# One layer trunk on one core: the c results of a block product in PSUM tiles of their own, no longer in the right half of the b tile

## The chip, the core and the metric

The kernel runs on one core of one Trainium2 chip. The metric is the time of one execution on the device in microseconds (us). Five engines work from queues of their own: TensorE (PE in the profile, with its weight loads as PEld), VectorE (DVE), ScalarE (ACT), GpSimd (POOL) and SyncE (SP, which issues most DMAs). Matmul results go to PSUM, and only DVE and ACT empty it here.

## The reference, cut to what matters

Two layers on 1024 tokens of width 1024, all in float32:

```
u = rms_norm(h);  proj = u @ w_in
mixed = concat(forgetting_attention(...), gated retention(...))
h = h + mixed @ w_out                                   # output projection
up = rms_norm(h) @ w_up                                 # 1024 x 5632
h = h + (gelu(conv(up[:, :2816])) * up[:, 2816:]) @ w_down
h = h + sigmoid(rms_norm(h) @ w_ple_gate) * (p @ w_ple_proj)
...
return rms_norm(h)
```

The change touches the products with w_out, w_up, w_down, and w_ple_gate of the first layer. The projections w_in, the attention, the retention, the embedding product and the gate of the second layer are left as they are.

## The kernel before, in words

Activations lie feature by token: a tile [128, 1024] holds 128 features of all tokens. Float32 precision is reached with two reduced parts, hi and lo, of each operand, and three matmuls (hi hi, hi lo, lo hi) for one product.

The four products named above go through `g_parts` (line 468). It computes a block of 256 output features by 1024 tokens, seen as a 2 x 2 matrix of 128 x 512 pieces c11, c12, c21, c22, with a scheme that needs seven multiplications of halves in place of eight. The seven are called parts and run in the order of NAMES (line 301): b0, c1, b1, c2, b2, a, b3. Parts b0 to b3 add up one after the other in one accumulator; each is emptied into the output pieces after it is computed, and the next goes on adding to what stands there. Parts c1 and c2 do so in a second accumulator, and part a stands alone. So b1 must wait until b0 has been emptied, b2 until b1 and b3 until b2 have, and c2 until c1 has.

Of PSUM there are two tiles `d` of 1024 columns (`dpsum`, line 175) and four tiles `s` of 512 columns (`spsum`, line 178). Before the change a block takes one d: its left half is the accumulator of the b parts, its right half that of the c parts. Part a takes an s. The attention's and retention's small products, and the statistics of the norms (`Stats.finish`, line 541), take tiles s too.

A part is 3 x len(moving) matmuls of 128 x 128 by 512 columns, where `moving` lists the pairs of contracted tiles: 2 in the output projection, 4 in up and gate, 3 or 2 in down. Over both layers there are 16 blocks of the output projection, 44 of up, 32 of down and 4 of the gate, 96 in all. `Joined` and `Stored` (lines 330 and 372) make the moving operands (x for part b0, xh and xl for the others) and `Fixed` (line 402) the weights (w, and wh and wl): sums of weights on POOL (tile ws), the hi part on ACT, the lo part on DVE. `Line` (line 445) loads and makes the weights of one block while the block before it is computed.

Emptying a part is `join` (line 496) where a product is added to h: one DVE addition of 128 x 512 for each piece. For the others it is `form` (line 503): b0 and b1 are copied by ACT (COPY), c1 by ACT with scale -1 (ACTIVATE), c2, b2 and a are added on DVE, and b3 is scaled into its piece on DVE. In the up stage the blocks named a (first half of up) and z (second half) take turns; in the gate they are named sg.

The code is traced in program order. The framework's scheduler then writes the queue of each engine, with a model of times (`schedule_with_timeline_sim=True`), and may move an instruction ahead of another on the same engine where no dependency and no tile forbids it; it writes the semaphore waits as well. SBUF is given out in 50 rooms and 6 half rooms (class Arena), and the order of their users is fixed. The output projection of a layer begins while the last retention pair is still running: `weave` mixes the two in the trace.

Of the kernel before, what the change touches and what calls it, by code (L numbers as in the profile page):

```python
# [19 lines left out]
T = 1024  # L20
# [139 lines left out]
def trunk(ctx, tc, ap):  # L160
# [11 lines left out]
    def G(name, dt=F32, shape=(P, T)):  # L172
        return arena.take(name, dt, shape)

    def dpsum():
        return ps.tile([P, T], F32, name="d", tag="d", bufs=2)

    def spsum():
        return ps.tile([P, 512], F32, name="s", tag="s", bufs=4)
# [54 lines left out]
    def weights():  # L234
        if len(ahead) < 2:
            fetch()
        return ahead.pop(0)
# [18 lines left out]
    def dense_fm(w, x):  # L256
        got = []
        for _ in g_dense_fm(w, x, got):
            pass
        return got[0]  # L260
# [207 lines left out]
    def g_parts(line, moving, evac, after=None):  # L468


        w = line.take()
        d = dpsum()
        for part, name in enumerate(NAMES):
            o = spsum() if name == "a" else d[:, 512:T] if name[0] == "c" else d[:, 0:512]
            more = name in ("b1", "b2", "b3", "c2")
            for p, x in enumerate(moving):
                whi, wlo = w.of(part, p)
                xhi, xlo = x.of(part)
                first, last = p == 0 and not more, p == len(moving) - 1
                nc.tensor.matmul(o, whi, xhi, start=first, stop=False, skip_group_check=more)  # L480
                nc.tensor.matmul(o, whi, xlo, start=False, stop=False, skip_group_check=more)
                nc.tensor.matmul(o, wlo, xhi, start=False, stop=last, skip_group_check=more)
                del whi, wlo, xhi, xlo
            evac(name, o)
            if part % 2 == 0:
                w.x[part // 2] = None
                if after:
                    after(part // 2)
                line.step()
            yield 0.7 * len(moving)  # L490

    def parts(*a):
        for _ in g_parts(*a):
            pass
# [413 lines left out]
    for l in range(DEPTH):  # L908
# [143 lines left out]
        def g_out():  # L1052

            nonlocal line, u, rb
            u = rb = None
            del pr[:], ret_tab[:]
            line = Line(specs())
            for p in range(2):
                mx.append(Joined(mixed[2 * p], mixed[2 * p + 1]))
                mixed[2 * p:2 * p + 2] = [None, None]  # L1060
            for q in range(4):
                for m in (2 * q, 2 * q + 1):
                    h[m] = G("h")
                    nc.sync.dma_start(h[m], h_dram[m])
                to = h[2 * q:2 * q + 2]
                yield from g_parts(line, mx, lambda name, s: join(name, s, to))
# [5 lines left out]
        for name in ("qs", "ks"):  # L1072
            d = dense_fm(weights(), u)
# [44 lines left out]
        for j in range(FC // 2):  # L1118
# [11 lines left out]
            for i in range(2):  # L1130
                c = G("conv")
# [9 lines left out]
            c = None  # L1141
# [6 lines left out]
            def after(n):  # L1148
                for m in u:
                    m.drop(n)  # L1150
                for m in stored[0]:
                    m.build(n)
                    if n < 3:
                        m.load(n + 1)
# [106 lines left out]
    for at, n in PIECES:  # L1261
        t = slice(at, at + n)
        pstats = Stats(n)
        for m in range(KC):
# [4 lines left out]
            d = dpsum() if m % 2 else spsum()  # L1269
# [3 lines left out]
            for i in range(parts):  # L1273
                c = slice(i * n // parts, (i + 1) * n // parts)
# [99 lines left out]
```

## Time and profile before

| | us |
|---|---|
| median of 3 runs | 3019.79 |
| lowest and highest | 3009.69 and 3020.57 |
| the profiled execution | 3013.45 |
| its span, first to last instruction | 3011.7 |

Stages, by what PE and DVE do: layer 0 attention and retention to about 502 us of the span, the output projection from 545 to 675 (until about 605 among the last of retention), up to 1147, down to 1425, gate to 1540; layer 1 attention to 2007, output projection to 2180, up to 2653, down to 2905, then the second gate and the final norm. In a row of the trace, every instruction has line 145, since a helper there records all of them, so rows are told apart by tile: `d<-xh,wh` is a matmul that writes a tile d from moving operand xh and weight wh. The idle time of an engine stands behind an instruction, with what ended it.

### The profile page before, as it was taken

How to read it: one execution, taken by the hardware profiler on the slowest of the kernel's cores; microseconds unless marked ns; L12 is line 12 of the kernel's file. 1: busy time of each engine (PE TensorE's matmuls, PEld its weight loads, DVE VectorE, ACT ScalarE, POOL GpSimd, SP SyncE). 2: the span in 40 equal slices, each digit the busy share in tenths (PEclk: the TensorE clock that was granted, in tenths of full speed). 3: DMA queues.
4: the chain of work that ended last, by engine and by line, in shares of the span. 5: the costliest groups of instructions: out<-in, count | busy, mean ns of one | idle time of the engine just before them, and what ended most of it. 6: DMA issues, size and time to landing. Idle time of an engine off the chain costs nothing.

```text
span 3011.7 us, 36343 instructions
## 1 busy us (share of the span) xinstructions
PE 2751.0 (91%) x13718; PEld 2257.8 (75%) x13718; DVE 2080.4 (69%) x3031; ACT 1227.8 (41%) x1824; POOL 885.5 (29%) x652
## 2 busy tenths in 40 slices
PE   8998999979999998997889889999699999989988
PEld 7887988747777776775678879887477777767766
DVE  4566656796777677779735656568967776777676
ACT  4454533453333333335434545334433333434252
POOL 2222232222332222333432222322223323223230
PEclk9999999989999998999999999999899999999999
DMA  5333123322332235433433331232222322364242
GB/s 154 85 85 91 45 80 100 106 88 74 109 107 93 88 126 192 142 104 108 169 104 85 85 91 45 80 106 96 87 84 98 112 88 94 137 207 129 84 140 95
DMA packets 116865, 315.77 MB, mean 105 GB/s; under 512 B 13521, under 2 KB 34513, under 8 KB 116689
## 3 DMA queue, kind: packets, MB, share of 16 engines
q1 hardware_dynamic: 113616, 305.05, 31.5%
q10 hardware_dynamic: 3072, 8.39, 1.2%
q8 instruction: 108, 1.77, 0.2%
q14 instruction: 69, 0.56, 0.1%
HBM read 210.04 MB, written 69.80 MB: 93 GB/s over the span
## 4 chain that ended last, share of the span: by engine, by line
PE 33%; DVE 12%; DMA 5%; issue 3%; ACT 3%; POOL 3%; SPq 0%; POOLq 0%; DVEq 0%; ACTq 0%
PE d L145 24%; PE s L145 8%; DVE wl L145 3%; POOL ws L145 2%; DVE xl L145 2%; DVE h L145 2%; DMA wr<-in_wup_dram 1%; DVE conv L145 1%; DVE t L145 1%; DMA zz<-zd 1%; ACT wh L145 1%; DVE ssq L145 1%; DMA wr<-in_wdown_dram 1%; DVE w L145 1%; DMA dr<-in_wtm_dram 0%
## 5 line engine op out<-in xcount | busy, mean ns | idle before, releaser
L145 PE MATMUL d<-xh,wh 128*128 128x512 f32 x1560 | 638.2, 409 | 81.8 <-DVE h L145 50.0
L145 PE MATMUL d<-xl,wh 128*128 128x512 f32 x1560 | 625.0, 401 | 0.2 <-DVE xl L145 0.2
L145 PE MATMUL d<-xh,wl 128*128 128x512 f32 x1560 | 623.9, 401 | 0.5 <-DVE wl L145 0.5
L145 POOL TENSOR_TENSOR ws<-wr 128x512 f32<-128x512 f32 (+2 forms) x192 | 267.3, 1401 | 1145.0 <-PE d L145 477.4
L145 PEld LDWEIGHTS d<-xh,wh 128*128 128x128 f32 x1560 | 299.4, 192 | 192.1 <-DVE h L145 52.0
L145 PEld LDWEIGHTS d<-xh,wl 128*128 128x128 f32 x1560 | 299.6, 192 | 72.6 <-DVE wl L145 1.5
L145 PEld LDWEIGHTS d<-xl,wh 128*128 128x128 f32 x1560 | 300.1, 192 | 65.8 <-DVE xl L145 0.6
L145 POOL TENSOR_TENSOR ws<-ws,wr 128x512 f32<-128x512 f32 (+2 forms) x192 | 270.8, 1411 | 129.1 <-issue 69.2
L145 PE MATMUL d<-x,w 128*128 128x512 f32 x936 | 243.2, 400 | 31.1 <-ACT w L145 12.0
L145 ACT CAST wh<-ws 128x1024 fp32r<-128x1024 f32 (+2 forms) x192 | 169.6, 888 | 229.5 <-POOL ws L145 220.6
L145 DVE TENSOR_TENSOR h<-h,d 128x512 f32<-128x512 f32 x288 | 194.8, 681 | 83.0 <-PE d L145 76.3
L145 DVE TENSOR_TENSOR wl<-ws,wh 128x1024 fp32r<-128x1024 f32 (+2 forms) x192 | 209.8, 1097 | 50.8 <-ACT wh L145 41.5
L145 PE MATMUL d<-dh,uh 128*128 128x256 f32 (+1 forms) x768 | 220.9, 289 | 19.7 <-DVE vst L145 10.3
L145 PEld LDWEIGHTS d<-x,w 128*128 128x128 f32 x936 | 174.7, 190 | 83.4 <-ACT w L145 18.3
L145 PE MATMUL d<-dl,uh 128*128 128x256 f32 (+1 forms) x768 | 220.0, 287 | 0.0
L145 PE MATMUL d<-dh,ul 128*128 128x256 f32 (+1 forms) x768 | 219.7, 287 | 0.0
L145 PE MATMUL d<-uh,dh 128*128 128x512 f32 (+1 forms) x584 | 197.2, 407 | 23.7 <-ACT dh L145 11.1
L145 POOL TENSOR_TENSOR dl<-dr,dh 128x1024 fp32r<-128x1024 f32 (+2 forms) x51 | 125.8, 2468 | 243.7 <-ACT dh L145 212.5
L145 PE MATMUL d<-ul,dh 128*128 128x512 f32 (+1 forms) x584 | 193.6, 398 | 0.6 <-DVE ul L145 0.6
L145 PE MATMUL d<-uh,dl 128*128 128x512 f32 (+1 forms) x584 | 190.7, 396 | 0.3 <-POOL dl L145 0.2
L145 PEld LDWEIGHTS d<-dh,uh 128*128 128x128 f32 x768 | 147.0, 192 | 22.2 <-DVE vst L145 10.7
L145 PE MATMUL s<-xh,wh 128*128 128x512 f32 x312 | 128.4, 413 | 35.9 <-ACT wh L145 26.0
(209 smaller groups left out, 5443.8 us busy)
## 6 DMA issues: line engine op xcount, KB each, us to landing
wr<-in_wup_dram SPq DMA_DIRECT2D x88, 512.0 KB, 3.6
zz<-zd SPq DMA_DIRECT2D x66, 512.0 KB, 4.1
wr<-in_wdown_dram SPq DMA_DIRECT2D x48, 384.0 KB, 4.0
zd<-z SPq DMA_DIRECT2D x66, 256.0 KB, 2.0
dr<-in_wqk_dram SPq DMA_DIRECT2D x32, 512.0 KB, 3.5
hs<-h SPq DMA_DIRECT2D x24, 512.0 KB, 2.6
h<-hs SPq DMA_DIRECT2D x24, 512.0 KB, 4.4
zd<-t SPq DMA_DIRECT2D x22, 512.0 KB, 2.6
```

The costliest lines, as they stand in the source:

```text
L145: ins = f(*[bare(v) for v in a], **{n: bare(v) for n, v in k.items()})
```

## The change

A block now takes only the left half of a d, for its b parts. Part c1 takes a tile s, which c2 uses again; part a takes another s, as before. The order in the trace, the matmuls and the emptying stay as they were. The right half of d is not used by blocks any more; the number of tiles d and s is unchanged.

```diff
         w = line.take()
-        d = dpsum()
+        b, c = dpsum()[:, 0:512], None
         for part, name in enumerate(NAMES):
-            o = spsum() if name == "a" else d[:, 512:T] if name[0] == "c" else d[:, 0:512]
+            if name in ("c1", "a"):
+                o = spsum()
+                c = o if name == "c1" else c
+            else:
+                o = c if name == "c2" else b
             more = name in ("b1", "b2", "b3", "c2")
```

## Rows read from the trace of the kernel before

**Rows 1.** The page's head: busy time of each engine with its share of the span and its instructions, and the shares of the chain that ended last by engine.

```profile
PE 2751.0 (91%) x13718; PEld 2257.8 (75%) x13718; DVE 2080.4 (69%) x3031; ACT 1227.8 (41%) x1824; POOL 885.5 (29%) x652
PE 33%; DVE 12%; DMA 5%; issue 3%; ACT 3%; POOL 3%; SPq 0%; POOLq 0%; DVEq 0%; ACTq 0%
```

**Rows 2.** The table by stretches: from and to, length, then busy us (and instructions) of PE, PEld, DVE, ACT and POOL, the granted clock of TensorE, the DMA share and GB/s. End of the output projection of layer 0, up of layer 0, last group of down of layer 0, end of the output projection of layer 1, up of layer 1.

```profile
600.00:675.00 75.00, 53.80 (x195) 36.34 (x193) 71.94 (x95) 37.47 (x53) 19.05 (x16) 0.91 0.25 88
675.00:1147.00 472.00, 441.71 (x1859) 347.70 (x1857) 345.44 (x343) 175.97 (x214) 143.83 (x89) 0.98 0.29 102
1366.00:1425.00 59.00, 41.49 (x145) 27.47 (x144) 58.65 (x76) 32.79 (x47) 20.46 (x14) 0.94 0.38 129
2105.00:2180.00 75.00, 54.40 (x193) 37.94 (x193) 71.20 (x94) 37.48 (x53) 19.35 (x16) 0.89 0.25 88
2180.00:2653.00 473.00, 443.72 (x1868) 349.62 (x1869) 351.70 (x348) 179.92 (x218) 144.92 (x89) 0.98 0.30 104
```

**Rows 3.** Waits of PE over the whole span: the tile that PE was to write, the engine and the tile it waited for, us in total, times, longest us.

```profile
PE d L145 <- DVE h L145: 54.0, 48, 4.6
PE s L145 <- ACT wh L145: 26.0, 21, 4.0
...
PE s L145 <- DVE wl L145: 13.0, 19, 1.5
...
PE s L145 <- ACT xh L145: 9.8, 5, 4.0
...
PE d L145 <- ACT z L145: 9.5, 14, 1.4
PE s L145 <- DVE xl L145: 9.0, 4, 4.1
...
PE d L145 <- ACT sg L145: 7.3, 5, 2.7
...
PE d L145 <- ACT a L145: 5.8, 10, 0.7
...
PE d L145 <- DVE z L145: 5.1, 7, 0.9
...
PE d L145 <- DVE a L145: 1.5, 2, 0.9
```

**Rows 4.** The same list for single stretches, the row of DVE's h alone, in this order: 502 to 605 (output projection beside retention, layer 0), 605 to 675 (its end), 1147 to 1366 (down of layer 0), 1366 to 1425 (its last group), 2007 to 2110 and 2110 to 2180 (output projection of layer 1, beside retention and its end), 2653 to 2905 (down of layer 1).

```profile
PE d L145 <- DVE h L145: 5.0, 5, 1.8
...
PE d L145 <- DVE h L145: 8.5, 6, 3.9
...
PE d L145 <- DVE h L145: 7.5, 10, 1.9
...
PE d L145 <- DVE h L145: 10.0, 7, 3.2
...
PE d L145 <- DVE h L145: 5.1, 5, 1.9
...
PE d L145 <- DVE h L145: 8.0, 5, 4.6
...
PE d L145 <- DVE h L145: 9.8, 10, 3.3
```

**Rows 5.** The order of time in the up stage of layer 0, from 741 to 764 us: start, duration, engine, operation, tiles, and in brackets the idle time before it with what ended it. Of a part of 12 matmuls only the first stands here.

```profile
741.49 0.58 ACT L145 COPY z<-d 128x512 f32<-128x512 f32 x1
742.69 0.39 PE L145 MATMUL s<-xh,wh 128*128 128x512 f32 x1
743.48 0.67 DVE L145 TENSOR_TENSOR a<-a,d 128x512 f32<-128x512 f32 x1
745.43 0.40 PE L145 MATMUL d<-xh,wh 128*128 128x512 f32 x1
751.18 0.60 ACT L145 ACTIVATE z<-d 128x512 f32<-128x512 f32 x1 [0.70 <-PE d L145]
751.66 0.68 DVE L145 TENSOR_TENSOR a<-a,d 128x512 f32<-128x512 f32 x1
751.84 0.50 PE L145 MATMUL d<-xh,wh 128*128 128x512 f32 x1 [0.69 <-ACT z L145]
754.94 0.59 ACT L145 COPY z<-d 128x512 f32<-128x512 f32 x1 [3.16 <-PE d L145]
763.24 0.67 DVE L145 TENSOR_TENSOR z<-z,d 128x512 f32<-128x512 f32 x1
763.96 0.50 PE L145 MATMUL d<-xh,wh 128*128 128x512 f32 x1 [0.74 <-DVE z L145]
```

**Rows 6.** Groups of instructions: line, engine, operation, tiles, shape and count, then busy us, mean ns of one, and the idle time before them with what ended it.

```profile
L145 PE MATMUL d<-xh,wh 128*128 128x512 f32 x1560 | 638.2, 409 | 81.8 <-DVE h L145 50.0
...
L145 DVE TENSOR_TENSOR h<-h,d 128x512 f32<-128x512 f32 x288 | 194.8, 681 | 83.0 <-PE d L145 76.3
...
L145 PE MATMUL s<-xh,wh 128*128 128x512 f32 x312 | 128.4, 413 | 35.9 <-ACT wh L145 26.0
```

**Rows 7.** All waits of all engines over the span, the largest: who waited, for whom, us in total, times, longest.

```profile
POOL ws L145 <- PE d L145: 526.0, 39, 28.9
```

**Rows 8.** The order of time beside retention in layer 0: the first and the last reading of one retention result in a tile s (its mean, and the result less its mean).

```profile
554.83 0.68 DVE L145 TENSOR_REDUCE gmean<-s 128x8 f32<-128x512 f32 x1
...
567.67 0.68 DVE L145 TENSOR_TENSOR yn<-s,gmean 128x512 f32<-128x512 f32 x1
```

## The prediction

> **What bounds the kernel now.** I read the page's totals first, then the table of stages, then who TensorE waited for, and last a stretch of the order of time. The totals say where to look: PE is busy for 2751 of 3011.7 us, and the chain that ended last gives PE 33% and DVE 12%, the largest two shares [rows 1]. So there are about 260 us of idle PE, and a change pays if it takes some of them away without adding others. In the up stage of a layer PE is idle for 30 us of 472, DVE for 127; in the end of the output projection, and in the last group of the down stage of layer 0, it is DVE that has nothing left: 71.9 of 75, 71.2 of 75 and 58.65 of 59 us [rows 2].
>
> The list of PE's waits has two kinds [rows 3]. Some are on operands (wh, wl, xh, xl: 26.0 + 13.0 + 9.8 + 9.0 = 57.8 us on the parts that go to s alone). The others are on the engine that empties PSUM: h by DVE 54.0, z by ACT 9.5, sg by ACT 7.3, a by ACT 5.8, z by DVE 5.1, a by DVE 1.5, together 83.2 us. Some 1.4 of the 54.0 belong to the last phase, which g_parts has no hand in (the window without it shows 9.8 us), so the pool that the change can touch is about 82 us, 2.7% of the span.
>
> **Do the two halves wait on each other?** All depends on this, and the order of time answers it [rows 5]. In that stretch z is the block that begins. Its b0 was emptied by the COPY at 741.49, over at 742.07. Its c1, in the other half, ended and was emptied by the ACTIVATE at 751.18, over at 751.78. At 751.84 PE starts a part that had been waiting for exactly that; the COPY at 754.94, started as that part ends, shows it to be b1. But b1 goes into b0's half, which had been empty for nearly 10 us: it waited for the other half. The same at 763.96: DVE's add at 763.24 empties one of c2 and b2, the next part of the block waits for it, and whichever of the two it is, its own half was emptied at 751.18 or 754.94. So in this build a tile's halves are handed back and forth as one thing. A block is a chain of six parts and six emptyings, b0 c1 b1 c2 b2 b3, and PE has work only because two blocks, with a tile d each, run side by side. That is seen too: at 742.69 PE takes part a of z, the later block, ahead of b2 of a at 745.43, which became free when DVE emptied c2 (743.48 + 0.67).
>
> The Trainium skill, "PSUM — Partial Sum Buffer", Summary: rules for kernel authors, says that to read PSUM while a matmul runs one should target another bank, and guard with semaphores by bank. By that, halves that are banks already would need no wait on each other, and the change would be worth 0 us. The wait of 0.69 us at 751.84 disagrees here, so the row decides.
>
> **The change part by part.** It removes the tie between b0, b1, b2, b3 and c1, c2. It adds no matmul, no evacuation, no DMA and no instruction on SP or POOL; the queues' order is written at build time by the framework's scheduler, which will order them anew once fewer things wait.
>
> 1. Ties. Of the five hand-overs within a block four cross the halves (b0-c1, c1-b1, b1-c2, c2-b2), and b2-b3 stays. So I take 4/5 of a wait where PE is the bound. Up stages: 9.5 + 5.8 + 5.1 + 1.5 = 21.9 us [rows 3]. Gate: 7.3 [rows 3]. Down, without the last group of layer 0: 7.5 + 9.8 = 17.3 [rows 4]. Output projection while retention still runs: 5.0 + 5.1 = 10.1 [rows 4]. Sum 56.6, of which 4/5 are 45.3 us. What covers the remaining true ties: b1 still needs b0 emptied, with c1 between. A part of 12 matmuls lasts 745.43 - 742.69 = 2.74 us [rows 5], hence 2.1 at 9 and 1.4 at 6, against 0.68 us for the emptying [rows 6]. It is covered unless DVE is late; in rows 5 DVE empties b2 of a only at 751.66, 3.3 us after the part's end. With that cover gone the next part that stalls is b1, then c2.
>
> 2. Where DVE is the bound, the remaining 10.0 + 8.5 + 8.0 = 26.5 us of waits [rows 4] can't all go: DVE has only 3.1 + 3.8 + 0.35 = 7.2 us to spare there [rows 2]. Between 0 and 7.2 I take the middle, 3.6.
>
> 3. The new place. c1 takes a tile of the ring s (four tiles), where a block took one and now takes two. If that tile is still held, c1's first matmul waits, and with it everything behind it on PE's queue, and then ACT and DVE that empty those parts. Bounds: 0 (in rows 3 the waits of s parts are on operands, not on an emptying), or one emptying of 0.68 us for each of 96 blocks = 65 us. Below 0 is excluded, since nothing is saved at this point. I take 0, the nearer row, because two blocks side by side need at most two c and two a, four in all.
>
> 4. Given back. A PE that runs ahead meets late operands. The weight sums on POOL wait 526 us in all for PE to free buffers [rows 7], so weights can't be made arbitrarily early, and 57.8 us of operand waits show what that looks like [rows 3]. On the other side a few of those waits exist only because PE took part a early for want of anything else. Bounds: nothing, or all of the gain. I take a third, by rows 2: in the up stages, which hold most of the matmuls, POOL is busy only 143.8 us of 472 and DVE 345, so there is room.
>
> Sum: 45.3 + 3.6 = 48.9, less a third (16.3), is 33 us. The profiled execution took 3013.45 us (span 3011.7 and 1.7 around it), 6.3 below the median of the three runs, 3019.8. It becomes about 2980, and the median about **2987 us**. Runs of the kernel before differ by up to 0.36%, so 0.5% (15 us) is about what can be told from no change.
>
> **Rivals.**
> - A, the change does nothing: the wait at 751.84 comes from something else that ACT did, and halves were separate all along. Both instances in rows 5 and the order of the parts speak against it. Time 3020. Chance 0.05.
> - B, the wait changes its name: PE goes ahead and stands before wh, wl or xl instead; of the 48.9 us three quarters or more come back. For it: 526 us of POOL behind PE [rows 7] and DVE at 73% of the up stage. Against: POOL at 30% there [rows 2]. Time about 3012. Chance 0.15.
> - C, slower: the ring s runs out where the output projection is woven with retention. A retention result held its s tile from before 554.83 (gmean) until DVE's yn at 567.67, over 13 us [rows 8], so with it, c and a held, one tile of four is left for retention's short products. Price: c held for about c1, b1, c2 and an emptying, 3 x 1.4 + 0.7 = 4.9 us, for four blocks in each layer: 39 us. It decides if it exceeds the gain by 15 us, that is if hardly half of the 48.9 us arrive. Then about 3040. Against it: only 8 of 96 blocks stand there, and other parts can fill in. Chance 0.10.
>
> The Trainium skill, "Perfetto Trace Analysis", Matmul Optimizations, asks that all 8 PSUM banks be used. The change leaves the right half of each d idle during blocks, so by that rule alone C would decide; no row here shows such a loss yet.
>
> **How the numbers follow.** Forecast 0.70, A 0.05, B 0.15, C 0.10. Faster by over 0.5%: 0.70. Within 0.5%: A and B, 0.20. Slower: 0.10. The forecast itself reaches from all 82 us gained (2938) to about 3004. The range goes on to A and B with the spread of the runs, 3026, and leaves out C and what lies below 2938.
>
> **What would show it.** Right: matmul rows by name shift from d to s (d<-xh,wh x1560 to x936, s<-xh,wh x312 to x936 [rows 6]); PE's waits on z, a and sg fall from 29.2 us to under 10, and those on h from 54 to about 30, the DVE-bound stretches keeping theirs; b1 starts while its block's c1 is not yet emptied; up stages end some 10 us shorter each. Step 4 is wrong if waits of PE on wh, wl, xh, xl grow by more than 16 us, step 3 if an s part waits for z, a, h or yn. The prediction falls altogether if b1 still waits for c1's emptying, or if new operand waits reach the size of the old ones.

## The result: 2902.3 us where 3015.0 were needed

The changed kernel takes 2902.29 us (median of 4 runs, 2898.59 to 2903.25), the kernel before 3014.98 beside it (4 runs, 3009.69 to 3020.57). The ratio is 0.9624, with a 95% interval of 0.9599 to 0.9648. The forecast was 2987, and its range ended at 2938. The direction was right, and 113 us came where 33 were expected.

### The profile after

The page's head, as in [rows 1].

```profile
span 2896.8 us, 36327 instructions
PE 2717.5 (94%) x13718; PEld 2263.5 (78%) x13718; DVE 2086.6 (72%) x3031; ACT 1226.5 (42%) x1824; POOL 902.0 (31%) x652
```

PE's idle time went from 3011.7 - 2751.0 = 260.7 us to 2896.8 - 2717.5 = 179.3, that is 81.4 less. The other 33.5 us of the 114.9 are *busy* time of PE, for the same 13718 matmuls. The page's groups, as in [rows 6]:

```profile
L145 PE MATMUL s<-xh,wh 128*128 128x512 f32 x936 | 377.8, 406 | 25.6 <-ACT wh L145 13.2
L145 PE MATMUL d<-xh,wh 128*128 128x512 f32 x936 | 374.8, 404 | 20.2 <-DVE h L145 12.6
```

The counts are those forecast, 936 and 936. The mean of one matmul is 406 and 404 ns, against 413 and 409. PE's waits over the whole span, as in [rows 3]:

```profile
PE d L145 <- DVE h L145: 17.8, 16, 2.7
...
PE s L145 <- ACT wh L145: 13.2, 10, 3.3
...
PE s L145 <- DVE xl L145: 11.2, 7, 3.0
...
PE d L145 <- ACT x L145: 8.8, 3, 4.1
PE s L145 <- DVE h L145: 6.8, 4, 2.5
...
PE d L145 <- DVE sg L145: 5.9, 2, 5.4
...
PE s L145 <- DVE wl L145: 5.7, 8, 2.7
PE s L145 <- ACT xh L145: 5.4, 2, 2.8
PE d L145 <- ACT w L145: 5.4, 4, 1.8
...
PE s L145 <- DVE yn L145: 3.5, 2, 1.8
...
PE d L145 <- ACT sg L145: 1.9, 2, 1.2
```

Waits on an emptying fell from 83.2 to 17.8 + 6.8 + 1.9 + 5.4 = 31.9 us; z and a are gone from the list. (Of the 5.9 us on DVE's sg, 5.4 are one emptying in the gate of layer 0; the other 0.5 is in the second gate, which the change leaves alone, and was there before.) Waits of s parts on operands fell as well, from 57.8 to 13.2 + 11.2 + 5.7 + 5.4 = 35.5, although far more parts now go to s. Those of d parts (w, x and their hi and lo parts) fell from 30.6 to 18.8. No operand wait was given back. The whole list, of which these are the rows that matter here, falls from 250.3 us in 215 stops to 169.9 us in 118.

The table by stretches, with the up stages cut at their own ends (from the first COPY of a piece of a to the last scaled piece of z), since every stage now starts earlier. After, layers 0 and 1:

```profile
671.80:1114.10 442.30, 434.56 (x1876) 351.15 (x1876) 352.26 (x349) 177.85 (x216) 145.70 (x89) 0.99 0.33 114
...
2119.40:2561.70 442.30, 434.13 (x1876) 351.19 (x1876) 352.96 (x349) 178.06 (x216) 146.75 (x89) 0.99 0.32 115
```

Before, cut in the same way:

```profile
680.10:1156.10 476.00, 447.14 (x1871) 352.06 (x1871) 349.44 (x347) 176.88 (x215) 143.83 (x89) 0.98 0.30 104
...
2184.60:2657.20 472.60, 444.39 (x1871) 349.97 (x1871) 351.30 (x347) 176.86 (x215) 144.92 (x89) 0.99 0.30 106
```

The up stages gave 33.7 + 30.3 = 64.0 us, of which idle PE is 21.1 + 20.0 and busy PE the rest. Cut by stage in this way, the down stages gave 35.4, the output projections 16.1, and the rest of the span next to nothing in sum; the attention of layer 1 even takes 8.7 us more (548.4 to 557.1).

The order of time in the up stage of layer 0 after, as in [rows 5]. x10 and x2 are matmuls in a row.

```profile
744.10 2.43 PE L145 MATMUL d<-x,w 128*128 128x512 f32 x10
...
749.15 0.63 PE L145 MATMUL d<-x,w 128*128 128x512 f32 x2
749.62 0.39 PE L145 MATMUL s<-xh,wh 128*128 128x512 f32 x1
749.82 0.59 ACT L145 COPY a<-d 128x512 f32<-128x512 f32 x1 [2.52 <-PE d L145]
...
752.40 0.40 PE L145 MATMUL s<-xh,wh 128*128 128x512 f32 x1
752.60 0.60 ACT L145 ACTIVATE a<-s 128x512 f32<-128x512 f32 x1 [2.19 <-PE s L145]
...
757.50 0.39 PE L145 MATMUL d<-xh,wh 128*128 128x512 f32 x1
...
760.46 0.59 ACT L145 COPY a<-d 128x512 f32<-128x512 f32 x1 [7.26 <-PE d L145]
```

Block a: b0 is the d<-x,w of 744.10 and 749.15 (another block's part stands between). Its c1 starts at 749.62, *before* the COPY that empties b0 has even begun; in the kernel before a c1 had to wait for the end of that COPY. No idle time stands on any PE row here. What the prediction had named as the sign, a b1 that starts before its block's c1 is emptied, does not occur in this stretch: b1 starts at 757.50, and the ACTIVATE that empties c1 is over at 753.20. The tie seen broken is that between b0 and c1. The Trainium skill, "Perfetto Trace Analysis", Matmuls, asks that independent groups rotate through banks so that the emptying of one overlaps the next group's matmuls; this is what these rows show. In the kernel before c1 had a bank of its own as well; the bank alone did not bring the overlap.

### The profile page after: what moved, and what is told of

Same layout as the page of the kernel before. It is cut to its first block, busy times and chain, and to the rows that moved or that the text cites. A ratio compares the mean times of both kernels' runs of the same rounds, so it can differ in the third digit from the quotient of the medians.

```text
span 2896.8 us, 36327 instructions
## 1 busy us (share of the span) xinstructions
PE 2717.5 (94%) x13718; PEld 2263.5 (78%) x13718; DVE 2086.6 (72%) x3031; ACT 1226.5 (42%) x1824; POOL 902.0 (31%) x652
## 5 line engine op out<-in xcount | busy, mean ns | idle before, releaser
L145 PE MATMUL s<-xh,wh 128*128 128x512 f32 x936 | 377.8, 406 | 25.6 <-ACT wh L145 13.2
L145 PE MATMUL d<-xh,wh 128*128 128x512 f32 x936 | 374.8, 404 | 20.2 <-DVE h L145 12.6
L145 PE MATMUL s<-xl,wh 128*128 128x512 f32 x936 | 377.4, 403 | 11.2 <-DVE xl L145 11.2
L145 PE MATMUL s<-xh,wl 128*128 128x512 f32 x936 | 372.0, 403 | 6.1 <-DVE wl L145 5.7
L145 PE MATMUL d<-xl,wh 128*128 128x512 f32 x936 | 373.6, 399 | 2.4 <-DVE xl L145 2.4
L145 PE MATMUL d<-xh,wl 128*128 128x512 f32 x936 | 370.6, 399 | 0.0
L145 DVE TENSOR_TENSOR wl<-ws,wh 128x1024 fp32r<-128x1024 f32 (+2 forms) x192 | 218.3, 1146 | 40.7 <-ACT wh L145 31.9
L145 PE MATMUL d<-dh,uh 128*128 128x256 f32 (+1 forms) x768 | 222.1, 290 | 22.8 <-DVE vst L145 11.2
L145 PEld LDWEIGHTS s<-xh,wh 128*128 128x128 f32 x936 | 180.0, 192 | 76.3 <-ACT wh L145 20.5
L145 PEld LDWEIGHTS s<-xl,wh 128*128 128x128 f32 x936 | 180.5, 193 | 54.8 <-DVE xl L145 14.3
L145 PEld LDWEIGHTS s<-xh,wl 128*128 128x128 f32 x936 | 180.0, 192 | 54.5 <-DVE wl L145 13.3
L145 PEld LDWEIGHTS d<-xh,wl 128*128 128x128 f32 x936 | 178.9, 191 | 42.2
```

The lines of the kernel that those rows point to most:

```text
L145: ins = f(*[bare(v) for v in a], **{n: bare(v) for n, v in k.items()})
```

## The experiments

Two questions. **Is it the ties between the halves** that cost the 113 us, or something else in the new form (the other tile, the place of part a)? And, since all named emptying waits together were only 83 us: **by what way do ties cost more than the waits they cause?** An emptying is ACT's or DVE's instruction that reads PSUM; the "true" ties are b0-b1, b1-b2, b2-b3 and c1-c2, the "false" ones b0-c1, c1-b1, b1-c2 and c2-b2. Each run has its own runs of the kernel before on the same chip (3009 to 3020 us), to which its ratio goes; times of different experiments, taken on different chips, can be compared to about 10 us. The edits are shortened: `...` and what stands in `<>` is paraphrased.

### 1. The ties put back on the changed kernel

```diff
+    FALSE = {"c1": "b0", "b1": "c1", "c2": "b1", "b2": "c2"}
...
+                for mm in (...the three matmuls...):
+                    if name in FALSE:
+                        tc.add_manual_dep(mm.ins, gone[FALSE[name]].ins.name, <semaphore>)
-            evac(name, o)
+            gone[name] = evac(name, o)
```

> The changed kernel, with the four cross ties of a block put back by hand: c1 waits until b0 is emptied, b1 until c1, c2 until b1, b2 until c2; c1 and c2 stay in a tile s of their own. Theory T (the ties between the halves are the cause): the gain goes, about 3015 us, within 10 of the kernel before, and each up stage is back at some 473 us. Theory R (the cause is the new place: with c in the ring s, which has four tiles, parts of later blocks can run ahead): about 2902 us as after the change.

Measured: 3033.65 us, ratio 1.0078 (1.0053 to 1.0103). The gain is gone, and 24 us more than that, where at most 10 were expected. PE's longest waits:

```profile
PE s L145 <- ACT a L145: 50.6, 22, 5.4
PE d L145 <- DVE h L145: 37.0, 27, 3.8
PE s L145 <- DVE h L145: 32.2, 21, 6.7
```

The new tiles alone bring nothing: with ties between two different tiles the emptying waits are back, and higher than before (these three rows make 119.8 us).

### 2. The ties taken away from the kernel before, tiles as they were

```diff
+        if name in FALSE:
+            tc.declare_no_dep(mm.ins, gone[FALSE[name]].ins)
+        if name in TRUE:   # b1: b0, c2: c1, b2: b1, b3: b2
+            tc.add_manual_dep(mm.ins, gone[TRUE[name]].ins.name, <semaphore>)
```

> The kernel before, c1 and c2 still in the right half of d, but the four cross ties are declared away and the true waits (b1 on b0's emptying, c2 on c1's, b2 on b1's, b3 on b2's) are put in by hand. Theory T: about 2902 us, within 15 of the changed kernel, up stages at some 442 us. Theory R: about 3015 us, since no place has changed.

Measured: 2887.44 us, ratio 0.9592 (0.9573 to 0.9612). That is 15 us below the change; by the ratios, whose intervals overlap, and by the two profiled spans (2885.4 against 2896.8 us) it is 10 to 11. c stands in the right half of d here, in a bank that the change leaves unused. With experiment 1 this shows the cause: the framework hands the two halves of one tile back and forth as one thing; a tile of its own is one way to end that, and here not the cheapest. 9.8 of the 11.4 us between the two spans lie between the attention of layer 1 and the end of its up stage (1123.4 against 1113.6 us). The place in the ring s is seen in the two output projections: the waits of s parts on h and yn (6.8 + 3.5 us), which all stand there after the change, are absent in experiment 2, and the two stages together take 5.3 us less. The largest piece, 7.7 us, is in the attention of layer 1, where hardly any blocks stand (557.1 against 549.4); what of it is due to the place is not shown. The Trainium skill, "Perfetto Trace Analysis", Matmul Optimizations, asks that all 8 banks be used: it was cited for rival C, and by experiment 2 it is right in sign, at no more than these 10 to 15 us, not the loss of rival C.

### 3. No ties, but every queue in its old order

Experiment 2, and the instructions of every engine held in the order of the kernel before (an order among instructions of one engine costs no semaphore).

```diff
+        for e, order in ORDER.items():          # read from the kernel before
+            for a, b in pairs(order):
+                tc.add_manual_dep(b, a.name, <same engine, no semaphore>)
```

> As the run with the ties declared away in place, and every engine's queue is held in exactly the order of the kernel before, so only the waits differ. Theory T1 (what pays is the waits themselves, at run time): PE's evacuation waits fall from 83 us to under 30 and the time to about 2930 us, with the operand waits on wh, wl, xh, xl left near 58 us. Theory T2 (what pays is the new order, in which the scheduler no longer takes part a early for want of other work): no more than 30 us gained, 2985 us or above.

Measured: 3002.60 us (10 runs), ratio 0.9973 (0.9963 to 0.9984): some 8 us of the 123. Of PE's waits, those on s parts and on h:

```profile
PE s L145 <- ACT wh L145: 50.4, 29, 4.2
PE s L145 <- DVE wl L145: 24.6, 18, 6.5
PE d L145 <- DVE h L145: 24.5, 19, 3.0
...
PE s L145 <- ACT xh L145: 12.4, 6, 3.9
PE s L145 <- DVE xl L145: 11.4, 4, 4.8
...
PE d L145 <- DVE a L145: 2.1, 2, 1.1
```

This is the run that answers the second question. Emptying waits: 24.5 + 2.1 = 26.6 us, 56.6 less than before, and no more than after the change. But operand waits on s parts are 50.4 + 24.6 + 12.4 + 11.4 = 98.8, 41.0 more, and those on d parts 35.0, 4.4 more. The whole list of PE's waits makes 248.1 us against 250.3. In the old order a wait that is taken away changes its name and comes back: 72% of it in operands of s parts, nearly all of it in the whole list. What the change gains it gains because the scheduler, once parts are free, *writes another order*.

### 4. The change in two of the four products

c has its own tile in up and gate only.

```diff
+        own = len(moving) == 4
-            if name in ("c1", "a"):
+            if name == "a" or name == "c1" and own:
```

> Only the blocks with four moving pairs (up and gate) get the changed places; output projection and down keep both halves of one d. If the stages add up, the time is that of before less 33.7 + 30.3 us in up and 4.0 in gate, as the two traces differ there: 3015 - 68 = 2947 us, and output projection and down last as before (131, 264, 132 and 248 us).

Measured: 2940.52 us, ratio 0.977 (0.9747 to 0.9792), near the 2947 expected. The gain is that of up: its stages take 440.6 and 441.5 us, 66.5 less than before, and the gate, for which 4.0 us were expected, gives 0.6. The two output projections and the down stage of layer 1 (246.4 us) are within 2 us of what they were. But stages that the edit leaves alone move too: the down stage of layer 0 takes 254.4 us, 10.0 less than before, and the attention of layer 1 takes 554.5, 6.1 more. So the stages add up only to within some 10 us.

### 5 and 6. Whose order? PE's held, or all others held

Experiment 3 with the old order for PE only, and for every queue but PE's.

```diff
+            if e != "PE": continue      # 5; in 6: if e == "PE"
```

> Ties declared away in place as before, but only PE's queue is held in the order of the kernel before; the other queues are ordered anew. The run with every queue held gave 3002.6 us, the one with none 2887.4. Theory O1 (the order of the parts on PE, in which a block's part a stands second and the next block begins with three parts of the old one left, is what costs): about 3000 us, operand waits of PE again above 80 us. Theory O2 (it is the order of weight making on POOL, ACT and DVE): about 2890 us.

> The opposite: DVE, ACT, POOL and SP are held in the order of the kernel before, PE is free. Theory O1: near 2887 us, at most 30 above. Theory O2: near 3000 us.

Measured for 5: 3010.78 us (10 runs), ratio 1.0000 (0.9986 to 1.0013). PE's old order alone takes the whole gain away. Its waits are those of experiment 3 in kind:

```profile
PE s L145 <- ACT wh L145: 42.2, 31, 4.1
PE s L145 <- DVE wl L145: 24.1, 18, 4.5
PE d L145 <- DVE h L145: 17.4, 20, 1.7
PE d L145 <- ACT w L145: 16.7, 14, 4.2
...
PE s L145 <- ACT xh L145: 14.7, 6, 4.9
```

Measured for 6: 3086.52 us, ratio 1.0257 (1.0229 to 1.0286), where at most some 30 us over experiment 2 were expected: a miss. Waits on ACT's z come first there:

```profile
PE d L145 <- ACT z L145: 44.0, 16, 4.5
PE d L145 <- DVE h L145: 34.3, 37, 4.6
PE s L145 <- ACT wh L145: 34.2, 19, 3.5
```

A new order of PE behind old orders of ACT and DVE is worse than either whole; the orders belong together. "PE's order pays" is true only with the others following it.

### 7. Part a early

In the old order part a often stands ahead of its block's c1, in the new one behind it. Experiment 2 with a forced ahead of c1 in up and gate:

```diff
+                if name == "a" and p == len(moving) - 1:
+                    for mm in c1_matmuls: tc.add_manual_dep(mm.ins, mms[2].ins.name, <no semaphore>)
```

> Ties declared away in place, all queues free, but in up and gate part a must stand ahead of c1, second in its block as in the kernel before; a new block still begins with two parts of the old one left. If part a standing early, ahead of its weights, makes the operand waits: up stages above 460 us and the whole above 2940 us. If it is the overlap of blocks: within 15 us of 2887.

Measured: 2890.45 us, ratio 0.9609 (0.9586 to 0.9632), the same as experiment 2. That the old order took a too early (step 4 of the prediction had this thought) is not, by itself, where the time lies. The run also shows that an order forced within one engine need not cost time in itself. For whole queues this is not shown: no run holds a kernel in its own order.

### 8. How far blocks overlap

In the old order a block begins while c2, b2 and b3 of the block before are still to come; in the new one c2 is done by then. First that overlap forced on experiment 2 (in up alone), then the other way, less overlap with the ties in place (up and gate of the kernel before):

```diff
+    LATES = ({"c2": "b0", "b2": "c1", "b3": "b1"}, {"b2": "b0"})   # part held behind that part of the next block; blocks take the two in turn
```

> Ties declared away in place (2887 us), queues free but for one thing: in the up stages c2 of a block must stand behind b0 of the next, b2 behind its c1 (or b0) and b3 behind its b1, so that two blocks overlap as in the kernel before. If it is this overlap that costs, at least half of the 64 us that up won is lost: 2920 us or more. If it is the fine order inside, within 15 us of 2887.

```diff
+                if name == "b0": ...                # on the kernel before: behind b2 of the block before
+                    tc.add_manual_dep(mm.ins, last_b2.ins.name, <no semaphore>)
```

> The kernel before, ties and halves as they were, but in up and gate the next block's b0 must stand behind b2 of the block before, as it does after the change. If the ties are what forces two blocks to overlap, PE now stands idle at the emptyings and the time is 3040 us or more. If the overlap alone were the harm and the ties cheap, below 2990 us.

Measured, overlap forced: 2911.93 us, ratio 0.9664 (0.9647 to 0.9682), 24.5 above experiment 2 and between the two marks set. The up stages take 463.0 and 453.8 us, against 443.9 and 443.0 in experiment 2 and 476.0 and 472.6 before. So this overlap costs 29.9 of the 61.7 us that up gave in experiment 2, about half; that the finer order is the rest was not tested.

Measured, less overlap with ties: 3139.34 us, ratio 1.0417 (1.0397 to 1.0437). The page's head, the waits, and the up stage of layer 0 in the table by stretches:

```profile
PE 2802.9 (89%) x13718; PEld 2284.1 (73%) x13718; DVE 2074.4 (66%) x3031; ACT 1226.0 (39%) x1824; POOL 881.1 (28%) x652
```

```profile
PE d L145 <- ACT z L145: 70.3, 24, 4.2
PE d L145 <- DVE h L145: 55.0, 52, 4.4
...
PE d L145 <- DVE a L145: 17.6, 22, 0.9
...
PE d L145 <- ACT a L145: 15.0, 22, 0.7
```

```profile
681.30:1217.70 536.40, 468.75 (x1876) 362.42 (x1876) 351.78 (x350) 176.82 (x216) 143.94 (x90) 0.94 0.27 93
```

With ties the far overlap was the scheduler's defence: without it PE stands at the emptyings. So the old order was better than this one *for tied halves*, and the worse one for free halves.

### 9. Are late weights what the old order suffers from?

Experiments 5 (old order of PE) and 2 (free order), both without the weight sums on POOL, then without most of the loading too. The four kernels work with wrong weights, since sums and loads are left out.

```diff
-                nc.gpsimd.tensor_tensor(v[:, 0, :], a[:, 1, :], b[:, 1, :], op=ALU.add)
-                nc.gpsimd.tensor_tensor(v[:, 1, :], v[:, 0, :], a[:, 0, :], op=ALU.add)
+                nc.gpsimd.tensor_tensor(v[:, :, 0:8], a[:, :, 0:8], b[:, :, 0:8], op=ALU.add)
+                v = v[:, :, 0:1].to_broadcast([P, 2, self.w])
...
-                nc.sync.dma_start(t, src[i])                          # third and fourth kernel
+                nc.sync.dma_start(t[:, :, 0:64], src[i][:, :, 0:64])
```

> PE's queue in the order of the kernel before with the ties declared away (3010.8 us), and the weight sums on POOL cut to 8 columns each; ACT and DVE read one column of them broadcast, so the products use wrong weights. If the old order costs because weights come late, the time falls by 70 us or more, to 2940 or less. If it costs in the moving operands or the emptyings, it stays above 2980.

> The same cut of the weight sums with PE's queue free (2887 us with the sums): the control for the run before. If weights are no bound in the new order, 2870 to 2887 us; more gained would say that the new order still waits for weights.

> As the run with PE's old order and the weight sums cut (2961.3 us), and of every weight tile of the block products only 64 of its columns are loaded; ACT and DVE read one column broadcast, so the products use wrong weights. What is left of the weight chain are its casts on ACT and DVE. If loads that arrive late are what the old order still pays for, the time falls by 50 us or more, to 2910 or less; if it is the casts in their queues behind the emptyings, it stays above 2940.

> The same cut with PE's queue free, the control (2855.1 us with the loads): 2840 to 2856 us, as operand waits of PE on weights are down to 4 us there in the up and down stages.

| | old order of PE | free order | difference |
|---|---|---|---|
| all work | 3010.78 | 2887.44 | 123.3 |
| without weight sums | 2961.28 | 2855.14 | 106.1 |
| and without most of the loads | 2922.62 | 2848.28 | 74.3 |

Ratios, in the order of the expectations: 0.9833 (0.9798 to 0.9867), 0.9476 (0.9456 to 0.9496), 0.9694 (0.9664 to 0.9724), 0.9442 (0.9420 to 0.9465). Both kernels in the old order fell between the marks set, and without sums the free order gained more than expected. So of the 123 us 17 go with the sums and 32 more with the loads, each to some 10 us. Leaving out the sums does more than bring weights sooner: DVE's busy time falls as well, from 2065.6 to 1941.2 us in the old order and from 2082.9 to 1943.4 in the free one, and the additions of conv, which read no weights, from a mean of 1462 to 1280 ns in the old order. So the 17 us are not shown to be late weights. Without the sums, waits on wh stay as they were; only without the loads do they fall. The row of the old order without sums, then of the old order without sums and loads:

```profile
PE s L145 <- ACT wh L145: 42.0, 32, 6.4
```

```profile
PE s L145 <- ACT wh L145: 14.1, 8, 4.5
```

Loads are therefore late in the old order, and the sums' own waits for a load agree: POOL's group of the first sums, in experiment 5 and in experiment 2.

```profile
L145 POOL TENSOR_TENSOR ws<-wr 128x512 f32<-128x512 f32 (+2 forms) x192 | 269.4, 1412 | 1133.2 <-PE d L145 505.7 <-DMA wr<-in_wup_dram 284.4 <-DMA wr<-in_wdown_dram 122.0
```

```profile
L145 POOL TENSOR_TENSOR ws<-wr 128x512 f32<-128x512 f32 (+2 forms) x192 | 282.6, 1478 | 1028.8 <-PE d L145 526.2 <-DMA wr<-in_wup_dram 191.8 <-DMA wr<-in_wdown_dram 75.7
```

284.4 + 122.0 = 406.4 us of waits for loads against 267.5. That buffers come free later in the old order, since parts of two blocks are interleaved over a longer stretch, would explain it; no run here isolates that. Where the remaining 74 us come from (the casts on ACT and DVE in their queues, the moving operands, the emptyings) was not settled.

### 10. More false ties taken away

Experiment 2, and the same between the halves of d in the two projections by token, which the change leaves alone.

```diff
+            for i in <matmuls into one half>:
+                for g in <the emptying of the other half>:
+                    tc.declare_no_dep(i, g)
```

> Ties declared away in place, and also between the halves of d in the token-major projections, where a half is emptied while the other is filled. If PE's waits on flog (12.4 us in all) and vst (11.6 us) are such ties and nothing takes their place, about 2887 - 24 = 2863 us; if they are true waits on a tile or turn into others, 2880 to 2890 us.

Measured: 2875.52 us, ratio 0.9560 (0.9538 to 0.9582), the fastest kernel that does all the work: 27 us under the change and 12 of the 24 us hoped for. The rest came back under other names, as the first of these waits of PE shows; it is 5.8 us in the changed kernel and in experiment 2.

```profile
PE s L145 <- DVE L L145: 13.7, 6, 5.0
PE d L145 <- ACT dh L145: 11.1, 3, 5.2
...
PE d L145 <- DVE flog L145: 2.0, 1, 2.0
```

## Why the prediction was right in sign and wrong in size

**"Do the two halves wait on each other?"** Right, and this carried the sign. Experiments 1 and 2 prove it from both sides, and c1 at 749.62 shows it in the trace. Rival A falls.

**Step 1, ties, and step 2, the DVE-bound ends.** Together 48.9 us less of emptying waits were forecast; it is 83.2 - 31.9 = 51.3. As an account of the named waits the steps were right, and so were their signs: waits on z, a and sg fell from 29.2 to 7.3 us, those on h from 54.0 to 24.6. Only the up stages, which were to end some 10 us shorter each, ended 33.7 and 30.3 shorter. As a *price* they failed: experiment 3 takes 56.6 us of them away and gains about 8.

**Step 3, the new place, priced at 0.** This was too low by a little. s parts do wait for h (6.8) and yn (3.5), the sign that the prediction named for being wrong here, and in the output projections, where rival C expected it. The two stages are 5.3 us longer than in experiment 2, where rival C priced 39; the whole kernel is 10 to 15 us longer. Rival C's mechanism was there and never decided.

**Step 4, given back.** This step failed, in sign. A third of the gain, 16.3 us, was to come back as operand waits; these fell by 57.8 - 35.5 = 22.3 on s parts and by 30.6 - 18.8 = 11.8 on d parts. The step took the order of the queues as given and asked what a PE that runs ahead would meet. For that order the reasoning holds, and more strongly than stated: 41.0 of 56.6 us come back on s parts alone in experiment 3, near the three quarters of rival B. But the prediction itself said that the scheduler would order the queues anew, and then priced nothing of it. The new order carries nearly the whole gain (experiments 3 and 5 against 2), though only with the ties gone (experiment 1).

**What no step had: PE's busy time.** It fell by 33.5 us at the same count of matmuls. "Busy" holds what is lost when PE is stopped and started. In the kernel before, the matmul after the one at 751.84 [rows 5] was

```profile
752.17 0.40 PE L145 MATMUL d<-xl,wh 128*128 128x512 f32 x1
```

It starts 0.33 us after the first, where matmuls in a row start 0.23 apart; and the last matmul before a stop counts with all of its 0.39 us. An estimate from these rows is 0.10 + 0.16 = 0.26 us of busy time for a stop, and 215 - 118 = 97 stops fewer make 25 of the 33.5 us. The rest is open. It is hardly the granted clock, whose mean over the span is 0.970 of full speed before and after. With more stops the clock comes in: in experiment 8 with less overlap, where PE stops most (254 times), busy time is 2802.9 us for the same work, and the mean granted clock in the up stage of layer 0 is 0.94, a mean of the two levels 1.2 and 2.4 GHz, against 0.99 after the change. The Trainium skill, "Perfetto Trace Analysis", Matmul Optimizations, says that TensorE scales its power with its use, so that matmuls should follow each other closely; these two rows agree. Reading idle time alone, as the prediction did, leaves all this out.

The account of the span then closes: 51.3 (emptyings) + 22.3 + 11.8 (operands of s and d parts) - 5.0 (all other waits of PE, which grew) + 33.5 (busy) = 113.9 of 114.9 us.

**A bound that would have held.** The range ended at 2938, at "all 82 us gained", as if the waits with that name were the most that could be had. A stage's own length says otherwise. In a dense stretch matmuls start about 0.23 us apart (2.74 us for 12 in [rows 5]; 752.40 - 749.62 = 2.78 for 12 after), and an up stage has 22 x 7 x 12 = 1848 of them, 425 us. Before, the two stages took 476.0 and 472.6 us: so by this estimate 51 and 48 us could be lost to *anything* that order and ties cause, not the 21.9 us that step 1 counted in both. The 64.0 us gained there lie within that bound; 17 us a stage are left.

## What to carry to other kernels

Where a scheduler writes the queues, a dependency can cost what the order written around it costs, not the waits that bear its name; bound what taking it away can bring by the stage's length less its matmuls times their pace. Look for false ties between halves of one PSUM tile even where little waiting shows, and end them by declaring the halves apart if that can be done, because a tile of its own takes a place from others (the output projections paid 5.3 us for it here). To see whether waits or order pay, hold the old order and take only the waits away.

## What had not been expected

The same 13718 matmuls are 2715 us of busy PE in the fastest kernel that does all the work and 2803 in the slowest; 88 us lie in how they are strung together. And removing waits that cost PE 56.6 us changed the time by 8 (experiment 3), while an order kept on four engines of five cost 199 us (experiment 6 against 2).
